# Gathering four blocks of tokens with sixteen matmuls in a row, in the gate projection's banks

## The chip, the cores and the metric

The kernel runs on one NeuronCore of a Trainium2 chip. The metric is the device time of one execution in microseconds (us); runs of a kernel are compared by their median. The profile is of one execution, and all times in it are us from the span's start unless marked ns.

## The reference

The program is one layer of a hybrid backbone over 512 latent tokens of 1024 channels with 256 context tokens: adaptive RMSNorm, one input projection, a bidirectional state-space scan and a gated MLP as parallel branches, an output projection, and then a mixture of experts. Only the last matters here:

```python
def expert_choice_ffn(xn, router_w, w_gate, w_up, w_down):
    b, n, d = xn.shape
    cap = CAPACITY_FACTOR * n // N_EXPERTS          # 64 tokens for each of 16 experts
    logits = jnp.einsum('bnd,de->ben', xn, router_w).astype(jnp.float32)
    aff = jax.nn.softmax(logits, axis=1)
    gate, idx = lax.top_k(aff, cap)
    xg = jax.vmap(lambda xs, ix: xs[ix])(xn, idx)
    hid = jax.nn.silu(jnp.einsum('becd,edf->becf', xg, w_gate)) * jnp.einsum('becd,edf->becf', xg, w_up)
    y = jnp.einsum('becf,efd->becd', hid, w_down) * gate[..., None].astype(xn.dtype)
    scatter = lambda ix, ys: jnp.zeros((n, d), ys.dtype).at[ix.reshape(-1)].add(ys.reshape(-1, d))
    return jax.vmap(scatter)(idx, y)
```

Each of the 16 experts picks 64 of the 512 tokens, runs a SwiGLU of width 1024 on them, and adds the weighted result back to these tokens. All weights are float32.

## The kernel before

All stages up to the router come first and are not touched. The expert stage runs over 8 pairs of experts (`for pr in range(NE // 2)`, L1129). The 128 tokens of a pair (64 for each expert) lie side by side as columns. For one pair, in the order of TensorE's queue:

- gate projection `pg = project("pg", ...)` (L1086): 8 steps `kt` over 128 input channels each; in every step four calls, for two halves of the 1024 outputs and two experts. One call is a matmul with 64 columns of weights loaded and 512 columns streamed; the trace shows each float32 call as two records. Between the steps the results of the pair before are added to their tokens (`to_their_tokens`, L1117, run from `between`).
- `route` (L1059): the pair's gate values and the transposed one-hot matrix `oh`.
- up projection `pu` (L1142), 64 records in a row; VectorE and ScalarE meanwhile form silu of the gate, and VectorE multiplies it by `pu` (L1144).
- the gather of the next pair's tokens, `channels` (L1074): for each of 8 blocks of 128 channels (`k`), four matmuls over the four tiles of 128 tokens (`x2`, shown as `F` in the trace) with the one-hot matrix `ot`, 128x128 each (eight records), and one ScalarE activation that scales and shifts the block with `mcol` and writes it to `xg` (shown as `m`). It comes in two halves of four blocks; behind each half stand four transposes of the hidden values (L1154) and a ScalarE copy of these into `ht` (L1155).
- the down projection `down` (L1156), two column halves of 32 records each, evacuated by VectorE (L1170) and split in two parts for the scatter.

The matmuls of this stage are kept in program order (`matmul`, L1042). PSUM has eight banks of 512 float32 columns: pool `pw` gives `x` two buffers, `pd` two, and `pg` and `pu` one buffer of two banks each. The four blocks of a half lie in one `x` bank, 128 columns apart, and the program lets TensorE write the next block to that bank only when ScalarE has read the last one.

For pair 0 there is no pair before it in which to gather. `first_tokens` (L1106) gathers two blocks ahead of every second step of the gate projection, and before step 6 also runs `places_of` (L1049), eight small matmuls that turn VectorE's top-k result into the slots of all other pairs.

Weights come by DMA from SyncE's queue (`expert_pieces`, L662, line L673 in the trace), in pieces of 1 MiB: 24 in a pair, two experts alternating, 8 for gate, 8 for up and 8 for down; in the last pair the down pieces are four of 1 MiB, four of 0.75 and four of 0.25. They go round 19 slots in SBUF (5 and 6 named `e`, 2 `w`, 6 `f`): a piece is requested when TensorE has read the last matmul of the piece 19 places before it. The first 19 are requested before the expert stage starts, the other 173 MiB as slots come free. Nothing else moves by DMA in this stage but the output at the end.

Of the kernel before, what the change touches and what calls it, by code (L numbers as in the profile page):

```python
# [7 lines left out]
F32 = mybir.dt.float32  # L8
# [4 lines left out]
AF = mybir.ActivationFunctionType  # L13
# [7 lines left out]
NT = 4  # L21
# [12 lines left out]
def tile_backbone(  # L34
# [7 lines left out]
    V, S, G, T = nc.vector, nc.scalar, nc.gpsimd, nc.tensor  # L42
# [127 lines left out]
    with tc.tile_pool(name="st", bufs=2) as st:  # L170
# [81 lines left out]
        for kt in range(NK):  # L252
            p = aux()
# [3 lines left out]
        for k2 in range(NK // 2):  # L257
            p = aux()
# [112 lines left out]
    for o, n, parts in ((0, 512, (xT,)), (512, 256, (xch.bitcast(F32), xcl.bitcast(F32)))):  # L371
        p = acc()[:, :n]
        ops = [(k, a) for k in (0, 4) for a in parts]
        for i, (k, a) in enumerate(ops):
            for q in range(4):
                T.matmul(p[32 * q:32 * q + 32, :], dtw[:, k + q, :], a[:, k + q, :],
                         start=i == 0, stop=i == len(ops) - 1)
        V.tensor_scalar(dth[:, o:o + n], p, dtb[:, 0:1], None, op0=OP.add)
    p = aux()
# [24 lines left out]
    p = aux()  # L404
# [11 lines left out]
    p = aux()  # L416
# [123 lines left out]
    def steps(gen, n):  # L540
        for _ in range(n):
            next(gen, None)
# [213 lines left out]
    for h in range(2):  # L756
        p = aux()
# [4 lines left out]
        p = aux()  # L762
# [7 lines left out]
    for m, wh, wl in ahead(cols(W, 3104)):  # L770
        pu = acc()
# [4 lines left out]
        for t in range(NT):  # L776
            T.matmul(pm[:, 128 * t:128 * t + 128], vt[:, t, 128 * m:128 * m + 128], wst[:, m, :],
                     start=True, stop=True)
# [15 lines left out]
    for m, is_gate, wh, wl in ahead(pairs(cols(W, 6176), cols(w_pb.rearrange("l k n -> (l k) n"), 0))):  # L794
        p = acc()
# [38 lines left out]
    for m, wh, wl in ahead(cols(W, 5152)):  # L834
        p = acc()
# [4 lines left out]
    for g in range(NG):  # L840
        p = aux()
# [8 lines left out]
    x2 = big.tile([128, NT, 1024], F32, name="F")  # L850
# [6 lines left out]
    for m, wh, wl in ahead(cols(w_pa.rearrange("l k n -> (l k) n"), 0)):  # L857
        p = acc()
# [17 lines left out]
    def full(name, bufs=1):  # L876
        return rp.tile([128, 1024], F32, name=name, bufs=bufs)
# [8 lines left out]
    mcol = rp.tile([128, 32], F32, bufs=1)  # L886
# [125 lines left out]
    pw = ctx.enter_context(tc.tile_pool(name="pw", bufs=2, space=PSUM))  # L1012
# [10 lines left out]
    p = pw.tile([128, 512], F32, name="pd")  # L1023
    for t in range(NT):
        T.transpose(p[:16, 128 * t:128 * t + 128], aff[:, t, :], ident)
    xg, ot = full("m1").rearrange("p (k n) -> p k n", k=NK), pick(rank)
# [15 lines left out]
    def matmul(*a, **k):  # L1042

        return tc.keep_in_program_order(T.matmul(*a, **k))  # L1044
# [4 lines left out]
    def places_of():  # L1049
        p = pw.tile([128, 512], F32, name="pd")  # L1050
        for k, a in enumerate((chosen, count)):
            for t in range(NT):
                matmul(p[:, 64 * k + 16 * t:64 * k + 16 * t + 16], a[:, 128 * t:128 * t + 128], i16,
                         start=True, stop=True)
        st_ = slott.rearrange("p t e -> p (t e)")
        S.copy(st_, p[:, :64])
        V.tensor_mul(st_, st_, p[:, 64:128])
# [13 lines left out]
        S.copy(oh, p)  # L1071
        return oh, gi

    def channels(xt_, ot, ks):  # L1074

        p = pw.tile([128, 512], F32, name="x")
        for j, k in enumerate(ks):
            o = p[:, 128 * j:128 * j + 128]
            for t in range(NT):
                matmul(o, x2[:, t, 128 * k:128 * k + 128], ot[:, t, :], start=t == 0, stop=t == NT - 1)  # L1080
            S.activation(xt_[:, k, :], o, AF.Identity, scale=mcol[:, 8 + k:9 + k], bias=mcol[:, k:k + 1])  # L1081

    def tokens():
        return full("m1").rearrange("p (k n) -> p k n", k=NK)
# [1 line left out]
    def project(name, op, between=lambda i: None):  # L1086
        p = pw.tile([128, 2, 512], F32, name=name, bufs=1)
        for kp in range(4):
            w = None
            for k in range(2):  # L1090
                kt = 2 * kp + k
                if pr == 0:
                    between(kt)
                w = w or [piece() for _ in range(2)]
                for hf in range(2):
                    for e in range(2):
                        matmul(p[64 * e:64 * e + 64, hf, :], op[:, kt, 64 * e:64 * e + 64],
                                 w[e][:, k, 512 * hf:512 * hf + 512], start=kt == 0, stop=kt == NK - 1)
                if pr:
                    between(kt)  # L1100
        return p

    fin = rp.tile([128, 8, NT], F32, name="rst")
    q = [fin[:, k, :] for k in range(8)]

    def first_tokens(kt):  # L1106
        if kt % 2 == 0:
            if kt == 6:
                places_of()
            channels(xg, ot, (kt, kt + 1))  # L1110

    def halves_of(hi, lo, c0, a):

# [14 lines left out]
    behind_ = iter(())  # L1128
    for pr in range(NE // 2):  # L1129
        last = pr == NE // 2 - 1  # L1130
        if pr == 0:
            pg = project("pg", xg, first_tokens)
        else:
            pg = project("pg", xg, lambda kt: steps(behind_, 1))
        oh, gi = route(pr, ot)
        if not last:
            ot = pick(slott[:, :, 2 * pr + 2:2 * pr + 4])
# [7 lines left out]
        if not last:  # L1145
            xg = tokens()
        ht = full("m2").rearrange("p (k n) -> p k n", k=NK)
        for hf in range(2):
            if not last:
                channels(xg, ot, range(4 * hf, 4 * hf + 4))  # L1150
            b = gs[hf]
            p = pw.tile([128, 512], F32, name="x")
            for k in range(4):
                transpose(p[:, 128 * k:128 * k + 128], b[:, 128 * k:128 * k + 128], ident)  # L1154
            S.copy(ht[:, 4 * hf:4 * hf + 4, :], p.rearrange("p (k n) -> p k n", k=4))  # L1155
        def down(c0, c1, nk, behind=None):  # L1156
            pd = pw.tile([128, 512], F32, name="pd", bufs=2)[:, :c1 - c0]
            for k0 in range(0, NK, nk):
                w = [piece() for _ in range(2)]
                with tc.issue_after(behind.ins) if behind and (k0 or c0 > 512) else nullcontext():  # L1160
                    for k in range(nk):
                        kt = k0 + k
                        for e in range(2):
                            (T.matmul if last else matmul)(pd[64 * e:64 * e + 64, :], ht[:, kt, 64 * e:64 * e + 64], w[e][:, k, :],  # L1164
                                     start=kt == 0, stop=kt == NK - 1)
            return pd
# [104 lines left out]
```

## Time and profile before

| | |
|---|---|
| time of the runs, median of 3 | 1179.45 us (1177.4 to 5647.97) |
| the profiled execution | 1177.17 us |
| its span, first to last instruction | 1175.4 us |
| TensorE (PE) busy | 1081.8 us, 92% of the span |
| weight loads (PEld), VectorE (DVE), ScalarE (ACT) | 61%, 49%, 29% |
| mean granted TensorE clock | 0.990 |

PE is TensorE's matmuls, PEld its weight loads, DVE VectorE, ACT ScalarE, SPq SyncE's DMA queue. Busy time is a union of the instructions' spans; matmuls are pipelined, so the end of one lies behind the start of the next. "x8" in a row counts merged records. In square brackets stands the idle time before an instruction and what released it.

### The profile page before, as it was taken

Reading aid. Unit: us, or ns where it says so; the run is one execution under the profiler, and the core shown is the slowest. Engines: PE = TensorE matmul, PEld = TensorE weight load, DVE = VectorE, ACT = ScalarE, POOL = GpSimd, SP = SyncE. Lnnn points to the kernel's source line nnn. Section 1 sums busy time; section 2 is a strip of 40 time slices with the busy share of each in tenths; the row PEclk is TensorE's granted clock in tenths of the full one; section 3 lists DMA queues with packets and bytes.
Section 4 is the critical chain, followed back from the end, with each engine's and each line's share of the span. In section 5 each row is a group of like instructions: output and inputs, shape, how many; then the busy total and the mean of one; then the engine's idle time right before and its main releaser. Section 6 shows DMA issues by size and latency. Waiting matters only on the chain.

```text
span 1175.4 us, 15016 instructions
## 1 busy us (share of the span) xinstructions
PE 1081.8 (92%) x5939; PEld 711.1 (61%) x5939; DVE 579.6 (49%) x1061; ACT 339.1 (29%) x645; POOL 66.4 (6%) x58
## 2 busy tenths in 40 slices
PE   2999899899999999999999699999898989899995
PEld 1778777799788888687897344343434343434333
DVE  2768999988797556536644711212030302121215
ACT  4343756553343223324333211010101010101002
POOL 2002232321000000100000000000000000000000
PEclk9999999999999999999999799999999999999998
DMA  9941624232576575525282898999999999999951
GB/s 213 248 121 54 200 90 161 73 108 73 179 219 210 191 241 186 173 74 177 72 326 97 298 374 314 395 406 393 407 393 409 393 408 396 405 397 402 402 182 72
DMA packets 149663, 291.85 MB, mean 248 GB/s; under 512 B 8468, under 2 KB 75188, under 8 KB 149592
## 3 DMA queue, kind: packets, MB, share of 16 engines
q1 hardware_dynamic: 149224, 290.79, 69.1%
q0 software_dynamic: 288, 0.07, 0.7%
q8 instruction: 47, 0.77, 0.3%
q14 instruction: 24, 0.20, 0.1%
q10 hardware_dynamic: 80, 0.02, 0.0%
HBM read 288.67 MB, written 2.18 MB: 247 GB/s over the span
## 4 chain that ended last, share of the span: by engine, by line
PE 78%; DVE 11%; ACT 4%; DMA 4%; issue 2%; POOL 0%; SPq 0%; DVEq 0%; ACTq 0%
PE x L1044 10%; PE pg L1044 10%; PE pu L1044 9%; PE pd L1044 8%; PE acc L358 7%; PE acc L360 7%; PE acc L359 7%; PE acc L603 2%; PE acc L601 2%; PE acc L602 2%; ACT m L1081 2%; DMA aw<-in_ada_w_dram 2%; PE pd L1164 1%; DVE gq L515 1%; DVE wl L74 1%
## 5 line engine op out<-in xcount | busy, mean ns | idle before, releaser
L358 PE MATMUL acc<-xmh,wh 128*128 128x512 f32 x352 | 139.1, 395 | 0.0
L359 PE MATMUL acc<-xml,wh 128*128 128x512 f32 x352 | 139.0, 395 | 0.0
L360 PE MATMUL acc<-xmh,wl 128*128 128x512 f32 x352 | 138.1, 392 | 0.0
L73 ACT CAST wh<-w 128x1024 fp32r<-128x1024 f32 (+1 forms) x84 | 84.4, 1005 | 170.5 <-PE acc L359 133.3
L74 DVE TENSOR_TENSOR wl<-w,wh 128x1024 fp32r<-128x1024 f32 (+1 forms) x81 | 95.8, 1183 | 68.2 <-ACT wh L73 67.2
L1170 DVE SCALAR_TENSOR_TENSOR t<-pd,gi,m 128x512 f32<-128x512 f32 (+2 forms) x17 | 12.2, 719 | 178.5 <-PE pd L1044 167.7
L1044 PE MATMUL x<-ot,F 128*128 128x128 f32 x512 | 74.9, 290 | 26.1 <-ACT m L1081 25.3
L1044 PEld LDWEIGHTS x<-ot,F 128*128 128x128 f32 x512 | 62.7, 193 | 44.1 <-ACT m L1081 36.6
L1125 DVE TENSOR_TENSOR F<-F,x 128x512 f32<-128x512 f32 x56 | 38.5, 688 | 91.2 <-PE x L1044 90.7
L1081 ACT ACTIVATE m<-x,mcol 128x128 f32<-128x128 f32 x64 | 29.3, 457 | 177.0 <-PE x L1044 177.0
L1044 PE MATMUL pg<-e,m 128*64 128x512 f32 x296 | 76.4, 602 | 0.0
L360 PEld LDWEIGHTS acc<-xmh,wl 128*128 128x128 f32 x352 | 66.3, 188 | 14.9 <-issue 1.2
L358 PEld LDWEIGHTS acc<-xmh,wh 128*128 128x128 f32 x352 | 66.3, 188 | 14.7 <-ACT wh L73 0.8
L601 PE MATMUL acc<-wh,xmh 128*128 128x256 f32 x256 | 73.5, 287 | 1.0 <-DVE F L614 1.0
L359 PEld LDWEIGHTS acc<-xml,wh 128*128 128x128 f32 x352 | 66.3, 188 | 13.1 <-issue 0.4
L603 PE MATMUL acc<-wl,xmh 128*128 128x256 f32 x256 | 73.3, 286 | 0.6 <-DVE wl L74 0.6
L1044 PE MATMUL pu<-e,m 128*64 128x512 f32 x304 | 73.7, 594 | 0.0
L602 PE MATMUL acc<-wh,xml 128*128 128x256 f32 x256 | 72.5, 283 | 0.0
L1044 PE MATMUL pd<-e,m 128*64 128x512 f32 x280 | 66.6, 594 | 0.0
L1144 DVE TENSOR_TENSOR t<-t,pu 128x512 f32<-128x512 f32 x16 | 10.3, 684 | 95.9 <-PE pu L1044 95.9
L358 PE MATMUL acc<-rh,wh 128*128 128x512 f32 x128 | 50.4, 396 | 0.8 <-ACT rh L73 0.5
L603 PEld LDWEIGHTS acc<-wl,xmh 128*128 128x128 f32 x256 | 49.0, 191 | 3.4 <-issue 2.5
(398 smaller groups left out, 1892.4 us busy)
## 6 DMA issues: line engine op xcount, KB each, us to landing
e<-in_w_up_dram SPq DMA_DIRECT2D x38, 1024.0 KB
e<-in_w_gate_dram SPq DMA_DIRECT2D x37, 1024.0 KB
e<-in_w_down_dram SPq DMA_DIRECT2D x35, 1024.0 KB
w<-in_w_in_dram SPq DMA_DIRECT2D x23, 1024.0 KB
f<-in_w_down_dram SPq DMA_DIRECT2D x20, 1024.0 KB
f<-in_w_up_dram SPq DMA_DIRECT2D x19, 1024.0 KB
f<-in_w_gate_dram SPq DMA_DIRECT2D x19, 1024.0 KB
e<-in_ada_w_dram SPq DMA_DIRECT2D x32, 512.0 KB
```

Source lines behind the costliest of these rows:

```text
L73: S.copy(hi, src)
L74: (lo_eng or V).tensor_sub(lo, src, hi.bitcast(F32))
L358: T.matmul(p, wh[:, kt, :], rh[:, kt, :], start=kt == 0, stop=False)
L359: T.matmul(p, wh[:, kt, :], rl[:, kt, :], start=False, stop=False)
L360: T.matmul(p, wl[:, kt, :], rh[:, kt, :], start=False, stop=kt == NK - 1)
L601: T.matmul(pp[t], lh[:, kt, a], wh[:, k, :], start=kt == 0, stop=False)
L602: T.matmul(pp[t], ll[:, kt, a], wh[:, k, :], start=False, stop=False)
L603: T.matmul(pp[t], lh[:, kt, a], wl[:, k, :], start=False, stop=kt == NK - 1)
L1044: return tc.keep_in_program_order(T.matmul(*a, **k))
L1081: S.activation(xt_[:, k, :], o, AF.Identity, scale=mcol[:, 8 + k:9 + k], bias=mcol[:, k:k + 1])
L1125: V.tensor_add(h[:, t, c0:c0 + 512], h[:, t, c0:c0 + 512], p)
L1170: V.scalar_tensor_tensor(a, pd, gi[:, 0:1], g2k[:, c0:c1], op0=OP.mult, op1=OP.mult)
```

## The change

`channels` takes a bank as an argument and issues all sixteen matmuls of four blocks first, then the four activations. The bank is no longer one of `x`: for the next pair's gather the two halves use the two banks of a `pg` buffer, for the first pair's those of a `pu` buffer. The two groups of transposes and their copies now stand together between the halves' matmuls. The first pair's eight blocks are all gathered ahead of the gate projection; `places_of` moves behind step 6's matmuls. `project` calls `between` behind a step's matmuls in every pair.

```diff
--- before.py
+++ after.py
@@ -1071,14 +1071,17 @@
         S.copy(oh, p)
         return oh, gi
 
-    def channels(xt_, ot, ks):
-
-        p = pw.tile([128, 512], F32, name="x")
-        for j, k in enumerate(ks):
-            o = p[:, 128 * j:128 * j + 128]
+    def channels(xt_, ot, hf, p):
+
+        for j in range(4):
+            k = 4 * hf + j
             for t in range(NT):
-                matmul(o, x2[:, t, 128 * k:128 * k + 128], ot[:, t, :], start=t == 0, stop=t == NT - 1)
-            S.activation(xt_[:, k, :], o, AF.Identity, scale=mcol[:, 8 + k:9 + k], bias=mcol[:, k:k + 1])
+                matmul(p[:, 128 * j:128 * j + 128], x2[:, t, 128 * k:128 * k + 128], ot[:, t, :],
+                       start=t == 0, stop=t == NT - 1)
+        for j in range(4):
+            k = 4 * hf + j
+            S.activation(xt_[:, k, :], p[:, 128 * j:128 * j + 128], AF.Identity, scale=mcol[:, 8 + k:9 + k],
+                         bias=mcol[:, k:k + 1])
 
     def tokens():
         return full("m1").rearrange("p (k n) -> p k n", k=NK)
@@ -1089,25 +1092,20 @@
             w = None
             for k in range(2):
                 kt = 2 * kp + k
-                if pr == 0:
-                    between(kt)
                 w = w or [piece() for _ in range(2)]
                 for hf in range(2):
                     for e in range(2):
                         matmul(p[64 * e:64 * e + 64, hf, :], op[:, kt, 64 * e:64 * e + 64],
                                  w[e][:, k, 512 * hf:512 * hf + 512], start=kt == 0, stop=kt == NK - 1)
-                if pr:
-                    between(kt)
+                between(kt)
         return p
 
     fin = rp.tile([128, 8, NT], F32, name="rst")
     q = [fin[:, k, :] for k in range(8)]
 
-    def first_tokens(kt):
-        if kt % 2 == 0:
-            if kt == 6:
-                places_of()
-            channels(xg, ot, (kt, kt + 1))
+    first_banks = pw.tile([128, 2, 512], F32, name="pu", bufs=1)
+    for hf in range(2):
+        channels(xg, ot, hf, first_banks[:, hf, :])
 
     def halves_of(hi, lo, c0, a):
 
@@ -1128,10 +1126,7 @@
     behind_ = iter(())
     for pr in range(NE // 2):
         last = pr == NE // 2 - 1
-        if pr == 0:
-            pg = project("pg", xg, first_tokens)
-        else:
-            pg = project("pg", xg, lambda kt: steps(behind_, 1))
+        pg = project("pg", xg, lambda kt: places_of() if pr == 0 and kt == 6 else steps(behind_, 1))
         oh, gi = route(pr, ot)
         if not last:
             ot = pick(slott[:, :, 2 * pr + 2:2 * pr + 4])
@@ -1145,14 +1140,17 @@
         if not last:
             xg = tokens()
         ht = full("m2").rearrange("p (k n) -> p k n", k=NK)
+        if not last:
+            gather = pw.tile([128, 2, 512], F32, name="pg", bufs=1)
+            channels(xg, ot, 0, gather[:, 0, :])
         for hf in range(2):
-            if not last:
-                channels(xg, ot, range(4 * hf, 4 * hf + 4))
             b = gs[hf]
             p = pw.tile([128, 512], F32, name="x")
             for k in range(4):
                 transpose(p[:, 128 * k:128 * k + 128], b[:, 128 * k:128 * k + 128], ident)
             S.copy(ht[:, 4 * hf:4 * hf + 4, :], p.rearrange("p (k n) -> p k n", k=4))
+        if not last:
+            channels(xg, ot, 1, gather[:, 1, :])
         def down(c0, c1, nk, behind=None):
             pd = pw.tile([128, 512], F32, name="pd", bufs=2)[:, :c1 - c0]
             for k0 in range(0, NK, nk):
```

How the instructions stand now. On TensorE, between the up and the down projection of pair 0 (`x` and `pg` are PSUM, `ot` the one-hot matrix, `F` the tokens, `ident` the transposes' identity; in brackets the engine whose semaphore is waited for), before, from the gather's third block to the first half's transposes:

```order
L1044 MATMUL x<-ot,F 128x128 [waits Activation_49]
L1044 MATMUL x<-ot,F 128x128 x3
L1044 MATMUL x<-ot,F 128x128 [waits Activation_49]
L1044 MATMUL x<-ot,F 128x128 x3
L1047 MATMUL x<-ident,t_5841 128x128 [waits DVE_49]
L1047 MATMUL x<-ident,t_5841 128x128 x3
```

And now, from the first of the gather to the first down matmul:

```order
L1044 MATMUL pg<-ot,F 128x128 [waits DVE_49,PE_49]
L1044 MATMUL pg<-ot,F 128x128 x15
L1047 MATMUL x<-ident,t_5838 128x128 [waits DVE_49]
L1047 MATMUL x<-ident,t_5838 128x128 x3
L1047 MATMUL x<-ident,t_5839 128x128 [waits DVE_49,Activation_49]
L1047 MATMUL x<-ident,t_5839 128x128 x3
L1044 MATMUL pg<-ot,F 128x128 [waits Activation_49]
L1044 MATMUL pg<-ot,F 128x128 x15
L1044 MATMUL pd<-f,m_5896 64x512 [waits DMAHW4_49,Activation_49]
```

Sixteen matmuls stand together where four stood, and the waits for ScalarE between blocks are gone. One is left on the second half's first matmul: by its semaphore count it is for the fourth activation of the first half. The wait ahead of the second transposes is for a ScalarE instruction of before the up projection, that ahead of the down projection for the first copy of `ht`.

On ScalarE at the same place, from the first block's activation to the first part of the scatter, before:

```order
L1081 ACTIVATE m_5898<-x,mcol 128x128 [waits PE_49,Activation_49]
L1081 ACTIVATE m_5898<-x,mcol 128x128 [waits PE_49] x3
L1155 COPY m_5899<-x 128x512 [waits PE_49]
L1081 ACTIVATE m_5898<-x,mcol 128x128 [waits PE_49] x4
L1155 COPY m_5899<-x 128x512 [waits PE_49]
L73 CAST t_5979<-t_5981 128x512 [waits DVE_49]
```

And now:

```order
L1083 ACTIVATE m_5895<-pg,mcol 128x128 [waits PE_49,Activation_49]
L1083 ACTIVATE m_5895<-pg,mcol 128x128 x3
L1151 COPY m_5896<-x 128x512 [waits PE_49] x2
L1083 ACTIVATE m_5895<-pg,mcol 128x128 [waits PE_49]
L1083 ACTIVATE m_5895<-pg,mcol 128x128 x3
L73 CAST t_5975<-t_5977 128x512 [waits DVE_49]
```

Only the first activation of four waits for TensorE (for the sixteenth matmul, by its count); the two copies stand together ahead of the second half's activations.

On TensorE at the start of pair 0, the sum of the rows before (with -) and now (with +):

```order
 L1025 MATMUL pd<-ident,aff 16x128 x4
-L1044 MATMUL x<-ot,F 128x128 x8
-L1044 MATMUL pg<-e,m_5697 64x512 x8
-L1044 MATMUL x<-ot,F 128x128 x8
-L1044 MATMUL pg<-e,m_5697 64x512 x8
-L1044 MATMUL x<-ot,F 128x128 x8
-L1044 MATMUL pg<-e,m_5697 64x512 x8
+L1044 MATMUL pu<-ot,F 128x128 x32
+L1044 MATMUL pg<-e,m_5697 64x512 x28
 L1044 LDWEIGHTS t_5717
```

The gather's 32 matmuls stand ahead of the gate projection, of which 28 now come before the slots' matmuls. SyncE's queue holds the same transfers in the same order.

## Rows read from the trace of the kernel before

**Rows 1.** The page: busy time; then DMA engines' busy tenths in 40 slices.

```profile
PE 1081.8 (92%) x5939; PEld 711.1 (61%) x5939; DVE 579.6 (49%) x1061; ACT 339.1 (29%) x645; POOL 66.4 (6%) x58
DMA  9941624232576575525282898999999999999951
```

**Rows 2.** Chain of waits, pair 1's up projection to down projection: start, us, what.

```profile
748.40 13.88 PE pu L1044 x64
762.28 1.10 PE x L1044 x8
...
775.75 13.88 PE pd L1044 x64
```

**Rows 3.** Timeline, pair 1's gather: start, us, engine, line, what, idle before.

```profile
762.21 1.16 PE L1044 MATMUL x<-ot,F 128*128 128x128 f32 x8
762.36 1.28 DVE L1144 TENSOR_TENSOR t<-t,pu 128x512 f32<-128x512 f32 x2 [12.11 <-PE pu L1044]
763.41 0.46 ACT L1081 ACTIVATE m<-x,mcol 128x128 f32<-128x128 f32 x1 [13.89 <-PE x L1044]
763.92 1.16 PE L1044 MATMUL x<-ot,F 128*128 128x128 f32 x8 [0.55 <-ACT m L1081]
...
768.33 0.60 PE L1047 MATMUL x<-ident,t 128*128 128x128 f32 x4
768.53 0.46 ACT L1081 ACTIVATE m<-x,mcol 128x128 f32<-128x128 f32 x1 [1.25 <-PE x L1044]
768.96 0.59 ACT L1155 COPY m<-x 128x512 f32<-128x512 f32 x1
769.04 1.16 PE L1044 MATMUL x<-ot,F 128*128 128x128 f32 x8
```

**Rows 4.** Window over pair 6's gather, L1044 alone: us, PE, PEld busy, clock, DMA.

```profile
1075.90:1089.40 13.50, 9.29 (x68) 7.77 (x66) 1.00 1.03 409
```

**Rows 5.** PE's timeline near the end; instructions of tile x (ns least/median/most).

```profile
1161.28 1.95 PE L1232 MATMUL pg<-ident,mcol 128*128 128x128 f32 x16
...
L1044 PE MATMUL x<-ot,F x512: 275/275/470, 657.5 to 1088.7; 128*128 128x128 f32 x171
```

**Rows 6.** Timeline of PE, and one row of DVE, in the first pair's gate projection.

```profile
657.45 1.96 PE L1044 MATMUL x<-ot,F 128*128 128x128 f32 x8
...
661.05 3.65 PE L1044 MATMUL pg<-e,m 128*64 128x512 f32 x16
...
677.40 0.35 PE L1044 MATMUL pd<-i,t 16*128 16x16 bf16 x8
...
684.06 1.05 PE L1044 MATMUL x<-aff,ot 128*128 128x2 f32 x8
...
670.09 1.21 DVE L1039 TENSOR_TENSOR_SCAN t<-t 16x512 bf16<-16x512 bf16 x1
```

**Rows 7.** Windows: us, PE, PEld, DVE, ACT, POOL busy, clock, DMA share, GB/s.

```profile
661.40:666.60 5.20, 4.65 (x26) 2.09 (x23) 4.98 (x11) 0.67 (x2) 0.00 (x0) 1.00 0.16 11
712.00:718.40 6.40, 6.40 (x36) 2.70 (x36) 0.00 (x0) 1.02 (x2) 0.00 (x0) 1.00 0.08 16
...
726.90:789.60 62.70, 59.30 (x296) 25.34 (x292) 11.97 (x19) 7.71 (x15) 0.00 (x0) 1.00 1.03 400
1040.60:1103.30 62.70, 59.30 (x294) 25.32 (x292) 11.97 (x19) 7.70 (x15) 0.00 (x0) 1.00 1.03 401
...
1132.50:1137.50 5.00, 5.00 (x26) 1.72 (x24) 0.00 (x0) 0.00 (x0) 0.00 (x0) 1.00 0.00 0
```

**Rows 8.** Chain of waits in the last pair's down projection: start, us, what.

```profile
1140.83 7.14 PE pd L1164 x32
...
1157.05 1.91 PE pd L1164 x28
```

**Rows 9.** Windows around the first block of the gather, columns as in rows 7.

```profile
650.00:657.40 7.40, 1.68 (x9) 0.97 (x8) 6.76 (x17) 0.31 (x1) 0.00 (x0) 0.50 1.04 392
...
659.40:660.00 0.60, 0.05 (x2) 0.04 (x1) 0.57 (x3) 0.46 (x1) 0.00 (x0) 0.97 1.01 403
```

## The prediction

> **What bounds the kernel now.** I read the page's busy shares and slices first. TensorE is busy 92% of the span, and in the last third of the span the DMA engines are 90% busy or more slice after slice [rows 1]. The change lies wholly in the expert stage, so two questions decide: which of the two ends last there, and what TensorE waits for.
>
> The chain of waits answers the first. Through the expert stage it runs on TensorE, and in each pair of experts it has the same piece between the last up matmul and the first down matmul: in pair 1 from 762.28 to 775.75, 13.47 us [rows 2]. The timeline of that piece [rows 3] is to be read row by row: a block of the gather (8 matmul records) starts at 762.21 and is over at 763.37; ScalarE evacuates it from 763.41 for 0.46; the next block starts at 763.92, released by that evacuation. Block follows block every 1.71 us. The four transposes at 768.33 fill part of one such wait. The window over pair 6 says that it is the same later: the gather 9.29 of 13.5 us busy, clock 1.00 [rows 4].
>
> How short could a block be? The sixteen 128x128 matmul records in a row at the end took 1.95 us [rows 5]; less one record's 0.275, that is 15 steps of 0.1117. Eight steps are 0.89, so 0.81 of each 1.71 is the wait, with the drain and refill that the idle column (0.55) leaves out.
>
> The second question is whether weights arrive in time. They move at 400 to 401 GB/s with the engines at 1.03 in the windows of pairs 1 and 6 [rows 7]: the transfers run at their own pace. But they are early: nothing moves any more from 1132.5 on, and the last weights are first used at 1157.05 [rows 7, 8]. TensorE is named by no row of the waits as waiting for a transfer in this stage. So TensorE ends last, with some 25 us in hand against the weights. That reserve is the second bound.
>
> **The change part by part.** *Gather of pairs 1 to 7* (seven times). Its 64 records and the 8 of the transposes stay; what changes is the number of waits. Counted from the first record: eight take 1.16 [rows 3], 24 more steps of 0.1117 make 3.84. By the built order the first evacuation waits for all sixteen matmuls, then four run without a wait. Evacuation to the next ScalarE row is 768.53 to 768.96, 0.43 [rows 3]; ScalarE starts 0.04 behind TensorE, so four end at 3.88 + 3 x 0.43 + 0.46 = 5.63. TensorE's eight transposes run meanwhile, to about 4.55. The second sixteen wait for the fourth evacuation although they write the other bank, and start at 5.68 (0.05 behind, as at 763.92): a new wait of 1.13 where there were seven, six of 0.81 and one of 0.38. Then 32 records to 9.36, and about 0.1 to the down matmul: 9.45 against 13.47, **4.02 us a pair, 28.1 in seven**.
>
> What is queued behind that wait: only the second half and the down matmuls. ScalarE's two copies for the down matmuls stand behind the four evacuations and end near 6.8 (2 x 0.59), before 9.45. The second half's evacuations end 1.8 behind it, under 13.88 us of down matmuls, so the next gate projection finds them. If that cover were gone they would cost 1.8. VectorE's products, the transposes' input, take 1.28 from 762.36 [rows 3] and are ready before 765.9, when they are now wanted.
>
> *First pair.* Before, 657.45 to 684.06, 26.6 us, the blocks two by two between gate matmuls with a wait in each two [rows 6]. Now: the first eight at half clock end at 659.41 as before; 24 more at 0.1117 to 662.3; four evacuations and a restart, to 664.1; 32 more, to 667.8; the 64 gate records, priced as the 64 of the up projection [rows 2], 13.9; the routing matmuls 0.3. End near 682.0: **2.1 saved**. VectorE has the routing's input by 671.3 [rows 6], so moving it behind a projection step costs nothing.
>
> *Sum for TensorE:* 28.1 + 2.1 = 30.2; the span would be 1145.2.
>
> *Weights.* Every slot is refilled when TensorE has read it, so the moved gather moves transfers too. The first gate pair was read by 664.7 (661.05 + 3.65) and the queue, dry until then, moved again from 666.6 [rows 6, 7]. Now that reading ends at 667.8 + 13.9/4 = 671.3 and the queue restarts near 673.5, 6.9 later (6.6 worked out, with a little for the first gate matmul's own start). In return it doesn't run dry again as it did from 712 to 718.4 [rows 7]: the slot that it lacked comes 6.1 us sooner, so it could go on at 712.3, and by then (38.8 us of transfers) 14.8 of the 16 pieces ahead are done. What lies behind the first 19 pieces is 173 MiB, 181.4 MB, at 400.5 GB/s 453.0 us without a gap: the last lands at 1126.5, which was 1132.5. The tightest piece is the second half of the last pair's first down part: 4 MiB (10.5 us) land behind it, so it lands at 1116.0. It was used half of 7.14 us behind 1140.83 [rows 8], 31.0 before the end. With that the span can't be under 1116.1 + 31.0 = **1147.1**. So TensorE alone would end 1.9 us sooner than the weights let it, and the weights decide by a hair.
>
> The profiled execution is 1177.17 with a span of 1175.4, 1.8 outside it; it lies 0.2 under the lowest run and 2.3 under the median shown. 1147.1 + 1.8 is **1149**, 28.2 less, 2.4%.
>
> The Trainium skill speaks against a gain here: DMA: Bandwidth & Descriptors, "Where 436 GB/s comes from", has HBM to SBUF bound near 358 GB/s. By that the 181.4 MB would take 507 us and the same sum would be 1201. The trace differs, 400 to 401 in the windows of both pairs [rows 7], and the measurement decides.
>
> **Unknown costs, from both sides.** No row shows 32 gather records in a row. Pace 0.1117 (sixteen in a row, rows 5) or 0.137 (1.10 for eight in the chain, rows 2, which holds a start): I take the first, being nearest in kind; the second takes 64 x 0.026 x 7 = 11.4 back. Nor does it show four evacuations in a row: 0.43 apart, or 0.51 with a hand-over like 763.37 to 763.41 each: 0.24 x 7 = 1.7 back. If the second sixteen waited for nothing, 1.1 x 7 more, but the weights then hold the span at 1147.1. Weights 1% slower than 400.5 (the pair windows differ by a quarter of that): 4.5 back. 1% faster: TensorE decides, 1147.0.
>
> **The rivals.**
> *A. The weights run slower once TensorE drains its reserve.* For it: the engines at 1.03 have no room, and at 1116 the reserve is gone. Against: their pace is the same in pairs 1 and 6. At 1 to 2% less, 1153.5 to 1158. With the Trainium skill's 358 it would be the 1201 above, which the trace all but rules out (0.01 of A's chance).
> *B. The gather is slower than the sum has it* (pace 0.137, or evacuations 0.51 apart): 30.2 - 11.4 = 18.8 saved, 1158; then the weights don't bind.
> *C. The transfers bind already and the gain is given back.* For it: DMA share 1.03. The time stays at 1177, or rises by the 6.9 of the late restart to 1184. Against: 25 us lie between the end of the transfers and the last first use [rows 7, 8].
> *D. Slower: TensorE's clock falls in the longer wait.* Before the gather it was busy 1.68 of the 7.4 us to 657.4, and the granted clock stood at 0.50, the lower of its two levels (1.2 of 2.4 GHz); it came back with the first block [rows 9]. If a wait of 1.1 (1.8 in the first pair) made it fall, the 72 records of a gather would take 0.1117 more each, 8.0 us, against 4.0 saved: 28 us more in seven, 1205. It decides from a half of the gather at the lower level on. Against: seven waits within 13.5 us now leave 1.00 in pair 6 [rows 4], and the total idle falls. The Trainium skill bears on this: TensorE: Matmul & The Clock Gate, "A second HAM failure mode: psum-queue depth-cycling", tells of short idles between matmul groups at which the clock swings. The trace of before, with its seven waits a pair, doesn't show it.
>
> **How the numbers follow.** Forecast 0.65 (1146 to 1152.5); A 0.13; B 0.11; C 0.06; D 0.05. Time 1149. The range reaches from 1145 (evacuations and weights both kind) over all of A and B to 1159, leaving out C and D, 0.11, and a little at each end. About 2%, 1153.6 and 1200.7, is what a measurement of this kernel can tell from no change. Faster by over 2%: the forecast, about half of A and a little of B, 0.75; within: the rest of A and B, C, 0.20; slower: D, 0.05.
>
> **What would show it.** In the changed trace: two runs of 32 gather records a pair, each near 3.8 us; four evacuations 0.43 to 0.46 apart; one TensorE wait of about 1.1 between transposes and the second run; last up to first down 9.4 to 9.5; pair period 58.7 instead of 62.7; DMA still near 400 GB/s and done near 1126; small TensorE waits on weights in the last pair alone. The forecast is wrong if a wait on weights stands before the last pair, if the 32 take 4.4, or if a clock under 1.00 stands between 670 and 1120.

## The result, and the profile after

The changed kernel takes 1150.36 us (median of four runs, 1149.88 to 1151.37), the kernel before 1177.4 beside it (median of its runs without one of 5647.97): ratio 0.977, 95% interval 0.975 to 0.980. That is 27 us and 2.3% less. The forecast was 1149.0 with a range of 1145 to 1159. The profiled execution is 1151.37, its span 1149.6.

The page of the changed kernel: busy times, the DMA slices, and the shares of the chain by engine.

```profile
PE 1070.2 (93%) x5939; PEld 709.5 (62%) x5939; DVE 579.2 (50%) x1061; ACT 331.9 (29%) x645; POOL 66.2 (6%) x58
...
DMA  9941634231476566622464669999999999999994
...
PE 74%; DVE 11%; DMA 7%; ACT 4%; issue 3%; POOL 1%; SPq 0%; DVEq 0%; ACTq 0%; POOLq 0%
```

TensorE's share rose by one point only; the last third of the slices is as full of transfers as in [rows 1].

The gather of pair 1 in the chain of waits, to be set against [rows 2]:

```profile
755.37 3.78 PE pg L1044 x32
759.16 0.02 issue
759.18 1.51 ACT m L1083 x4
760.69 0.04 issue
760.73 3.84 PE pg L1044 x32
764.57 0.57 PE pd L1044
```

From 755.37 to 764.57 are 9.20 us where 13.47 stood: 4.27 saved in this pair, 29.9 in seven. TensorE's and then ScalarE's timeline of the same piece, against [rows 3] (idle time and its releaser in brackets):

```profile
755.30 3.84 PE L1044 MATMUL pg<-ot,F 128*128 128x128 f32 x32
758.98 1.04 PE L1047 MATMUL x<-ident,t 128*128 128x128 f32 x8
760.73 3.84 PE L1044 MATMUL pg<-ot,F 128*128 128x128 f32 x32 [0.72 <-ACT m L1083]
```

```profile
759.18 1.50 ACT L1083 ACTIVATE m<-pg,mcol 128x128 f32<-128x128 f32 x4 [16.57 <-PE pg L1044]
760.56 1.08 ACT L1151 COPY m<-x 128x512 f32<-128x512 f32 x2
764.61 1.50 ACT L1083 ACTIVATE m<-pg,mcol 128x128 f32<-128x128 f32 x4 [2.97 <-PE pg L1044]
```

Thirty-two records take 3.84 and four evacuations 1.50; one wait is left, 0.72 in its row.

The first pair, TensorE's timeline, against [rows 6]:

```profile
655.90 5.78 PE L1044 MATMUL pu<-ot,F 128*128 128x128 f32 x32
663.33 3.84 PE L1044 MATMUL pu<-ot,F 128*128 128x128 f32 x32 [1.64 <-ACT m L1083]
...
681.42 1.05 PE L1044 MATMUL x<-aff,ot 128*128 128x2 f32 x8
```

From the first gather record to the routing matmuls are 25.5 us (681.42 - 655.90) where 26.6 stood. The first 32 records needed 5.78, the second 3.84. The windows say why, and how the transfers went (columns as in [rows 7]; the last three are the granted clock, the DMA share and GB/s):

```profile
657.00:660.00 3.00, 3.00 (x16) 3.00 (x15) 2.86 (x7) 0.00 (x0) 0.00 (x0) 0.50 0.58 223
660.00:661.00 1.00, 1.00 (x11) 1.00 (x10) 0.96 (x2) 0.00 (x0) 0.00 (x0) 0.93 0.00 0
661.00:673.00 12.00, 10.36 (x67) 6.21 (x67) 8.38 (x17) 3.00 (x8) 0.00 (x0) 1.00 0.06 16
720.00:778.50 58.50, 57.78 (x294) 24.97 (x292) 11.96 (x19) 6.88 (x15) 0.00 (x0) 1.00 1.03 401
1012.00:1070.60 58.60, 57.88 (x294) 25.07 (x292) 11.95 (x19) 6.89 (x15) 0.00 (x0) 1.00 1.03 401
1130.00:1132.00 2.00, 2.00 (x26) 1.46 (x24) 0.54 (x1) 0.00 (x0) 0.00 (x0) 1.00 0.00 0
```

The clock stood at 0.50 (1.2 of 2.4 GHz) for four microseconds of the gather. The transfers were all but at rest from 661 to 673, then ran at 401 GB/s as before, and were done by 1130, where 1126 was forecast. A pair takes 58.5 us now, so TensorE uses up its reserve of weights and meets them in the last pair. Its timeline there:

```profile
1101.18 3.22 PE L1044 MATMUL pu<-e,m 128*64 128x512 f32 x13 [0.91 <-DMA e<-in_w_up_dram]
...
1106.30 3.65 PE L1044 MATMUL pu<-w,m 128*64 128x512 f32 x14 [1.47 <-DMA w<-in_w_up_dram]
...
1118.51 3.65 PE L1162 MATMUL pd<-f,m 128*64 128x512 f32 x16 [1.57 <-DMA f<-in_w_down_dram]
```

The last pair, from its first gate matmul in the chain (1070.78) to the end, takes 78.8 us; before it was 72.1. So the span's 25.8 us come together as 29.9 from seven gathers, 1.1 from the first pair, 1.6 from a stage that began sooner in this execution (655.90 against 657.45, an early part that the change doesn't touch), and -6.7 for weights.

### The profile page after: what moved, and what is told of

Same layout as the page of the kernel before. It is cut to its first block, busy times and chain, and to the rows that moved or that the text cites. A ratio compares the mean times of both kernels' runs of the same rounds, so it can differ in the third digit from the quotient of the medians.

```text
span 1149.6 us, 15045 instructions
## 1 busy us (share of the span) xinstructions
PE 1070.2 (93%) x5939; PEld 709.5 (62%) x5939; DVE 579.2 (50%) x1061; ACT 331.9 (29%) x645; POOL 66.2 (6%) x58
## 4 chain that ended last, share of the span: by engine, by line
PE 74%; DVE 11%; DMA 7%; ACT 4%; issue 3%; POOL 1%; SPq 0%; DVEq 0%; ACTq 0%; POOLq 0%
PE pg L1044 15%; PE pu L1044 10%; PE pd L1044 8%; PE acc L358 7%; PE acc L360 7%; PE acc L359 7%; PE x L1044 4%; PE acc L603 2%; PE acc L601 2%; PE acc L602 2%; DMA w<-in_w_up_dram 2%; DMA aw<-in_ada_w_dram 2%; DVE wl L74 1%; ACT m L1083 1%; DVE gq L515 1%
## 5 line engine op out<-in xcount | busy, mean ns | idle before, releaser
L1044 PE MATMUL pg<-e,m 128*64 128x512 f32 x296 | 76.0, 602 | 0.0
L1044 PE MATMUL pu<-e,m 128*64 128x512 f32 x304 | 74.8, 595 | 0.9 <-DMA e<-in_w_up_dram 0.9
L1044 PE MATMUL pd<-e,m 128*64 128x512 f32 x280 | 66.6, 594 | 0.0
L1083 ACT ACTIVATE m<-pg,mcol 128x128 f32<-128x128 f32 x56 | 21.0, 456 | 135.9 <-PE pg L1044 135.9
L1044 PEld LDWEIGHTS pg<-ot,F 128*128 128x128 f32 x448 | 51.1, 192 | 12.5 <-ACT m L1083 6.8
L1044 PE MATMUL pg<-ot,F 128*128 128x128 f32 x448 | 53.7, 279 | 5.1 <-ACT m L1083 5.1
```

What stands on the lines that cost most here:

```text
L1083: S.activation(xt_[:, k, :], p[:, 128 * j:128 * j + 128], AF.Identity, scale=mcol[:, 8 + k:9 + k], bias=mcol[:, k:k + 1])
```

## The experiments

Theory W: the gathers and the first pair save TensorE more than the time shows, and the weights take the rest back in the last pair. Rival R: the time follows TensorE's saving, and the last pair is longer for another reason. All ratios are to the kernel before on the same chip.

| kernel | median us | ratio, 95% interval |
|---|---|---|
| changed kernel again | 1151.18 | 0.978, 0.976 to 0.980 |
| pairs only | 1150.68 | 0.978, 0.976 to 0.981 |
| first pair only | 1173.85 | 0.998, 0.996 to 1.000 |
| no wait for the second sixteen | 1150.63 | 0.978, 0.976 to 0.981 |
| changed, half the weights' bytes | 1143.26 | 0.971, 0.969 to 0.973 |
| no wait, half the bytes | 1135.26 | 0.965, 0.963 to 0.967 |
| before, half the bytes | 1175.29 | 0.998, 0.997 to 1.000 |
| single banks | 1151.27 | 0.978, 0.975 to 0.980 |
| first pair two blocks ahead | 1146.39 | 0.973, 0.971 to 0.976 |
| the same, no wait | 1145.64 | 0.974, 0.971 to 0.976 |
| the same, TensorE kept busy ahead | 1143.67 | 0.972, 0.970 to 0.974 |
| changed kernel, third time | 1148.65 | 0.975, 0.973 to 0.978 |

### The changed kernel again, and its two parts

> The changed kernel once more, beside its parts. Expected: 0.977 of before, 1150 us. Theory W (the weights cap the end): the gather of each of seven pairs is 4.3 us shorter on TensorE and the first pair's piece 1.0 us, but the last pair takes 78.8 us from its first gate matmul to the end where it took 72.1, waiting for its up and down pieces. If the first pair's matmuls again take 5.8 us for the first 32 records with the granted clock back only 4 us behind their start, that is the change's own doing and not one run's; if they take 4.9, it was chance.

Measured: 1151.18. The first 32 records took 5.54; in all eight traces of kernels with this first pair it was 4.83 to 6.06. So the slow start is neither a constant nor one run's mishap: it depends on how long after the gather's first record the clock comes back.

For the pairs alone the first pair stays in its old form, with `between` ahead of the step in pair 0:

```diff
-    first_banks = pw.tile([128, 2, 512], F32, name="pu", bufs=1)
-    for hf in range(2):
-        channels(xg, ot, hf, first_banks[:, hf, :])
+    def first_tokens(kt):
+        if kt % 2 == 0:
+            if kt == 6:
+                places_of()
+            channels2(xg, ot, (kt, kt + 1))
```

> The change in the seven later pairs alone; the first pair gathers two blocks at a time between gate matmuls, as before. Theory W: TensorE loses the 1.0 us that the first pair gained, but the first gate pieces are read at about 665 instead of 671, so the weights start to move again some 6 us sooner; they may run dry for 2 or 3 us near 712. The last pair then waits 3 us or more less, and the time is 1147 to 1149, at or below the changed kernel. Rival R (the time follows TensorE's saving, the waits of the last pair come from something else): 1.0 more than the changed kernel, 1151.5.

Measured: 1150.68 (1149.03 to 1152.67), the changed kernel's time as far as the runs can tell. The 1147 to 1149 that I had drawn from theory W did not come: the restart did come sooner, but it bought nothing. The window of 70 us from the first gather record, of the changed kernel and then of this one:

```profile
655.90:725.90 70.00, 67.58 (x375) 34.52 (x376) 21.16 (x40) 10.20 (x24) 0.00 (x0) 0.97 0.83 324
```

```profile
655.73:725.73 70.00, 67.02 (x361) 33.55 (x362) 20.11 (x39) 10.87 (x24) 0.00 (x0) 0.95 0.85 322
```

324 and 322 GB/s: in the same time as much was moved. With the old first pair TensorE reads the gate pieces over 28.7 us (this execution's first gather record to routing, again with a late clock), so the queue ran dry again between them (DMA share 0.38 from 660 to 670, 0.90 and 0.92 in the two tens behind it, 0.82 from 710 to 720). So theory W is to be counted from how many bytes have moved by the time the queue stays full, and not from when it starts. I read this out of the run after its result; the versions at the end put it to the test.

> The change in the first pair alone; the seven later gathers go block by block as before. Both theories: the weights have 25 us in hand, so the restart of the transfers that comes 6 us later costs nothing, and the time is that of before less 1.0, some 1177 to 1178 (ratio 0.998 to 1.000). If the later restart cost something by itself, 1180 to 1184 (ratio above 1.002).

The edit is the other half of the diff. Measured: 1173.85, ratio 0.998 (0.996 to 1.000), some 2.4 us less than before and more than the 1.0 expected. In the three traces with the old first pair the stretch from first gather record to routing is 26.6, 28.7 and 28.3; in the eight with the new one 24.6 to 25.8, 25.2 in the mean. The mean saving is 2.6, and the profiled pair with its 1.1 was the odd one. A restart that is late does no harm while 25 us are in hand.

### Is it the weights? The wait taken away, and the bytes halved

```diff
-            channels(xg, ot, 1, gather[:, 1, :])
+            channels(xg, ot, 1, pw.tile([128, 2, 512], F32, name="pu", bufs=1)[:, 1, :])
```

> The changed kernel with the second sixteen matmuls of each later gather in a buffer of their own (the up projection's, free by then), so that they no longer wait for the four evacuations of the first. Both: the TensorE wait between the transposes and the second sixteen (0.72 us of idle column, 1.0 with the refill) goes and last up to first down falls from 9.2 to about 8.2 us, in seven pairs. Theory W: the weights set the end, so the last pair waits 7 us longer and the time stays at that of the changed kernel, within 1 us. Rival R: 7 us less, 1143.

Measured: 1150.63, the changed kernel's time. The chain of waits in pair 1 has the two runs of 32 records with only the transposes between them:

```profile
750.92 3.77 PE pg L1044 x32
754.69 0.87 PE x L1047 x8
755.56 3.57 PE pu L1044 x32
759.13 3.15 PE pd L1044 x13
```

From 750.92 to 759.13 are 8.21 us where the changed kernel had 9.20. But TensorE's timeline now shows it waiting for weights in pair 6 already:

```profile
1034.84 3.66 PE L1044 MATMUL pu<-e,m 128*64 128x512 f32 x16 [0.94 <-DMA e<-in_w_up_dram]
1039.98 3.65 PE L1044 MATMUL pu<-e,m 128*64 128x512 f32 x14 [1.48 <-DMA e<-in_w_up_dram]
```

One microsecond less in each of seven gathers, and not one in the time: what TensorE saved, it waits for weights a pair earlier. That is theory W.

```diff
+                    n += 1
+                    nl = nk if n <= 19 else nk // 2
-                    load(w, dram(exw[m], (e * 1024 + k * 128) * 1024 + c0,
-                                 [[1024, 128], [128 * 1024, nk], [1, c1 - c0]]))
+                    load(w[:, :nl, :], dram(exw[m], (e * 1024 + k * 128) * 1024 + c0,
+                                 [[1024, 128], [128 * 1024, nl], [1, c1 - c0]]))
+                    w = Half(w, nl)
```

`Half` lets the matmuls of step k read step k % nl of the piece.

> The changed kernel with half the bytes of every expert piece behind the 19th left out (half of those weights are not loaded; the matmuls read the loaded half twice, in the same number and shape). Theory W: the waits of the last pair vanish, it takes 72.1 us again instead of 78.8, and the time is 1150.4 less 6.7, that is 1143 to 1144.5; every gather is as in the changed kernel. Rival R (the last pair is longer for another reason than the weights' lateness): 1150, with the last pair near 78.

> The same half of the bytes left out, and the second sixteen matmuls in a buffer of their own, without the wait. Theory W: with the weights out of the way the removed wait shows in the time: 1.0 us in each of seven pairs less than with half the bytes alone, 1136 to 1137.5. Rival (the wait's time turns up elsewhere on TensorE, for instance in the down matmuls waiting for ScalarE's copies): no gain, 1143 to 1144.

> The kernel before with the same half of the bytes left out. Theory W: the weights set nothing there, 25 us in hand, so the time stays within 1 us of before, 1177 to 1179. Rival C (transfers bind already, or their traffic slows TensorE or the evacuations): 1170 or less. The difference between this and the changed kernel with half the bytes is then TensorE's whole saving, 33 to 34 us by theory W (30.9 from the gathers and about 1.5 to 2 that differ from run to run).

Measured: 1143.26, 1135.26 and 1175.29. With half the bytes the changed kernel is 7 us faster, in the expected band, and no transfer stands in its chain in the last pair:

```profile
1091.00 13.91 PE pu L1055 x64
1104.91 0.02 issue
1104.93 0.70 DVE t L1150
```

The 64 up records now run in one piece of 13.91, and the last pair takes 70.8 us instead of 78.8. Without the wait as well it is 8.0 us faster again, 0.7 below the band: the microsecond per gather that was worth nothing above is paid once the weights are out of the way. The kernel before gains 1.4 (0.998, 0.997 to 1.000); I had said within 1. Its last pair is 1.3 shorter (70.8), and the chain of waits shows the place: 42 down matmuls in a row ahead of the scatter, where the kernel before has 32 [rows 8] and then the evacuation of these by VectorE.

```profile
1139.02 9.02 PE pd L1175 x42
1148.04 0.43 PE pg L1199
```

So 1.3 of the gain in each of these kernels is another order at the end (those matmuls aren't held in program order) and not the weights; 6.7 of the 8.0 remains for these. Theory W stands and R falls.

### The banks

```diff
-            gather = pw.tile([128, 2, 512], F32, name="pg", bufs=1)
-            channels(xg, ot, 0, gather[:, 0, :])
+            channels(xg, ot, 0, pw.tile([128, 512], F32, name="x"))
...
-            channels(xg, ot, 1, gather[:, 1, :])
+            channels(xg, ot, 1, pw.tile([128, 512], F32, name="x"))
```

> The changed kernel with the sixteen matmuls of each later gather in the two single banks that the transposes use too, instead of the gate projection's pair. Sixteen in a row and four evacuations stay. Expected: the second four transposes now wait for the first half's evacuations and the second sixteen for the copy of the first transposes, about 0.5 us more a gather (9.7 instead of 9.2), 3.5 in seven; by theory W the weights hide that and the time is that of the changed kernel, 1150 to 1151. Rival (the choice of banks carries the gain): the gather is back above 12 us and the time above 1165.

Measured: 1151.27. TensorE's timeline of pair 1 in this kernel:

```profile
756.59 3.84 PE L1044 MATMUL x<-ot,F 128*128 128x128 f32 x32
760.26 0.60 PE L1047 MATMUL x<-ident,t 128*128 128x128 f32 x4
762.02 0.66 PE L1047 MATMUL x<-ident,t 128*128 128x128 f32 x4 [1.16 <-ACT m L1083]
762.51 3.71 PE L1044 MATMUL x<-ot,F 128*128 128x128 f32 x31
```

The gather takes 9.68 (756.66 to 766.34 in the chain), 0.5 more than in the changed kernel as worked out; the weights cover it. Sixteen in a row carry the shorter gather (13.47 before), the banks half a microsecond a pair that the time doesn't show.

### A version that beats both

If the weights set the end, the first pair is the place: what it delays, all later pieces have late. The first version gathers two blocks at a time into `x` banks, always two blocks ahead of the gate matmuls that use them (`blocks` is sixteen records and two evacuations):

```diff
+    def two_more():
+        k = next(ahead, None)
+        if k is not None:
+            blocks(xg, ot, (k, k + 1), pw.tile([128, 512], F32, name="x"))
+
+    two_more()
+    def first_tokens(kt):
+        if kt % 2 == 0:
+            two_more()
+            if kt == 6:
+                places_of()
```

> The later pairs as in the changed kernel; the first pair gathers two blocks at a time into banks of their own, always two blocks ahead of the gate matmuls that read them, so that TensorE waits for no evacuation there. Theory W (the weights set the end, counted from when their queue stops running dry): routing comes 23.8 us behind the first gather record instead of 25.6, the first gate pieces are read 9.3 us behind it instead of 15, the transfers start again 5 us sooner, lose about 1 us by running dry once more, and the time is 1145.5 to 1147. Rival, from the run with the first pair as before (its transfers started sooner as well, ran dry again and gave no gain): the queue runs dry again until the up pieces are read, nothing is gained, 1150 to 1151.

> The same first pair, and the later gathers' second sixteen in a buffer of their own, without the wait for the evacuations. Theory W: TensorE's further 7 us go into waits for weights, and the time is that of the version with the first pair alone, within 1 us (1145 to 1147). Rival: 7 us less than that one, 1139.

Measured: 1146.39 and 1145.64, as theory W had it; the two agree within 1 us although the second has the wait taken away in seven gathers, which was worth 8.0 us with half the bytes. The changed kernel beside them took 1148.65, so the gain over it is 2.3 and 3.0 us; the runs of the first (1143.66 to 1147.7) lie all below its runs (1148.06 to 1154.15), those of the second (1144.66 to 1148.85) overlap with them a little. TensorE's timeline of the first:

```profile
654.02 5.06 PE L1044 MATMUL x<-ot,F 128*128 128x128 f32 x32
659.01 3.65 PE L1044 MATMUL pg<-e,m 128*64 128x512 f32 x16
662.60 2.05 PE L1044 MATMUL x<-ot,F 128*128 128x128 f32 x16
664.58 3.65 PE L1044 MATMUL pg<-e,m 128*64 128x512 f32 x16
```

No bracket, so no wait; the first gate pieces are read 8.6 us behind the first gather record. Its window of 70 us moved 350 GB/s for the changed kernel's 324:

```profile
654.02:724.02 70.00, 69.22 (x383) 34.20 (x384) 21.57 (x41) 10.41 (x24) 0.00 (x0) 0.98 0.91 350
```

That is 1.8 MB more, 4.5 us of transfers at 401 GB/s; from the first gather record to the end this execution takes 490.0 us, the changed kernel's three 493.2 to 494.1.

The third version is the second with twelve matmuls on the identity behind the last matmuls ahead of the wait:

```diff
+    busy = aux()
+    with tc.issue_after(row.ins):
+        for _ in range(12):
+            T.matmul(busy[:, 0:128], ident, ident, start=True, stop=True)
```

> The last version, with twelve matmuls of the identity by itself (24 records, read by nobody) in the wait of 5.7 us ahead of the first gather. It tests the term of the first pair that was mis-sized: there the first 32 records took 4.8 to 6.1 us from run to run where 3.84 is the pace at full clock. If TensorE's being busy ahead of the gather brings the granted clock to 1.00 by its start, the first sixteen records take 1.95 to 2.1 us instead of 3.3 to 4, everything behind, the restart of the transfers too, comes about 2 us sooner, and the time is 2 us under the version before. If the clock stays at 0.50 until it has come back by itself: no change, or 0.5 us more.

> The changed kernel beside the three versions on the same chip: 0.978 of before, 1150 to 1151 us; 493 to 494 us from the first gather record to the end of the span.

Measured: 1148.65 for the changed kernel, 1.4 below the 1150 to 1151 expected of it, and 1143.67 (1143.14 to 1146.58) for this version beside it (1148.06 to 1154.15): 5.0 us or 0.4% less, and the runs of the two don't overlap. It is 2.0 under the version without the idle work, as expected, but the runs of these two overlap (1144.66 to 1148.85 without it), so this difference is not shown by the times alone. In the two profiled executions the stretch from the first gather record to the end is 486.2 us instead of 491.3. Its timeline and its windows:

```profile
649.05 3.56 PE L1014 MATMUL aux<-ident 128*128 128x128 f32 x24
654.98 0.60 PE L1029 MATMUL pd<-ident,aff 128*16 128x128 f32 x4 [2.37 <-DVE t L1007]
655.70 3.81 PE L1048 MATMUL x<-ot,F 128*128 128x128 f32 x32
```

```profile
649.00:650.00 1.00, 1.00 (x7) 1.00 (x6) 0.96 (x4) 0.00 (x0) 0.00 (x0) 0.50 1.01 389
650.00:651.00 1.00, 1.00 (x9) 1.00 (x8) 0.93 (x3) 0.00 (x0) 0.00 (x0) 0.73 1.04 389
651.00:652.00 1.00, 1.00 (x11) 1.00 (x10) 0.90 (x3) 0.00 (x0) 0.00 (x0) 1.00 1.06 389
653.00:655.60 2.60, 0.60 (x4) 0.30 (x4) 2.45 (x7) 0.00 (x0) 0.00 (x0) 1.00 1.05 385
655.70:725.70 70.00, 70.00 (x390) 33.65 (x392) 21.95 (x42) 10.42 (x24) 0.00 (x0) 1.00 0.94 363
```

The clock rose during the idle work and held over the 2.37 of waiting behind it, the first 32 records took 3.81 where they took 5.98 without the idle work, and the 70 us moved 363 GB/s instead of 349.

## Why the prediction was right, step by step

**The gather.** The pace taken from the sixteen records at the end [rows 5] was exact: 3.84 for 32. The wait that the built order showed was there. It came out shorter since four evacuations took 1.50, 0.35 apart, where I had 0.43 from an evacuation followed by a copy [rows 3]: 1.75. TensorE sat idle 0.72 and not 1.13, and a pair saved 4.27 and not 4.02. Both bounds that I had kept lay on the dear side; that an evacuation could follow its own kind faster than a copy follows an evacuation I didn't weigh.

**The first pair.** 2.1 was forecast, 1.1 seen in the profile, 2.6 in the mean of all traces. That the size was near is luck: I let the clock come back 2.0 us behind the first record because it had done so in one execution [rows 6, 9], and so had 4.85 us for the first 32 records. It came back 4.2 us behind it here, and the 32 records took 4.83 to 6.06. The old first pair was late in the same way in two of its three traces, so that the difference came out near all the same.

**TensorE alone** would therefore have ended sooner than the 1145.2 of the span forecast. With half the bytes the time is 1143.3, or 1144.6 with the 1.3 of the other order put back, against 1145.2 + 1.8 = 1147.0 by my sum.

**The weights.** That they would decide was the step that made the forecast good: by TensorE alone it would have come to 1144.6, nearly 6 us under what came. But "by a hair", 1.9 us of waiting, was mis-sized: 6.7 went to them. One part of this is that TensorE was quicker than the sum; that moves the wait and not the end. The other is the term "lands at 1116.0", and it does move the end. I took it from the bytes at the mean pace, and by bytes it came at 1115.1. That this is 0.9 sooner is luck again: the stage began 1.6 sooner in this execution, and the transfers started again at 672.0 and not at 673.5. A piece, though, is there when the last of the sixteen DMA engines has moved its share, and these had drifted apart. The sixteen landings of that piece (the trace records when each engine's share lands) lie between 1113.6 and 1118.5, the eighth at 1115.0; TensorE started again at 1118.51. With the 31.0 us behind it that gives 1149.5, and the span is 1149.6. In eight of the nine traces in which TensorE waits for weights the span ends 31.1 us behind the last landing of this piece, in the ninth (two blocks ahead, no wait) 32.7. Counted from the restart, the piece was there 446.5 us later where my sum had 442.5: 4.0 too late, of which the early start hid 1.5. In the same way an up piece, first share at 1102.8 and last at 1106.3, released the matmuls at 1106.30; the chain of waits names it:

```profile
1087.81 18.45 DMA w<-in_w_up_dram
```

How far the sixteen landings of one piece lie apart, mean over the pieces of a pair (24, in the last 28), and the most in the last pair:

| kernel | pairs 1 to 3 | pair 6 | last pair | most in it |
|---|---|---|---|---|
| before | 1.4 to 1.7 us | 2.3 | 2.2 | 2.3 |
| changed | 1.6 to 1.9 | 3.3 | 3.9 | 4.9 |
| first pair two blocks ahead | 2.6 to 2.8 | 4.1 | 4.6 | 5.7 |

The Trainium skill has the mechanism: by DMA: Bandwidth & Descriptors, "Why a DMA increments its semaphore by 16 and not by 1", every engine reports its own share and only all sixteen reports mean that the data is there. The landings in the trace agree (last one at 1118.46, TensorE at 1118.51); how far they lie apart is this case's number.

Why they drift apart was not tried by an experiment. It is not that the queue has no rests: in the kernel before the transfers ran at a share of 1.03 and 401 GB/s from 721 to 1103 too, and their landings stayed within 2.5 us. The trace shows that the drift grows in steps. In the changed kernel it goes from 1.8 to 3.2 us at 900.4 and from 3.5 to 4.8 at 1113.1, just ahead of the tightest piece; each step comes just behind a transfer of 16 KB that takes 1.1 us, at 896.3 and 1109.9, in the queue that the page lists as

```profile
q8 instruction: 47, 0.77, 0.3%
```

(packets, MB, share of the engines). In the eleven traces with all bytes, each of the 22 steps of over 0.4 us from one piece to the next, from 730 us on, comes within 4.4 us behind such a transfer; most of these transfers, some 26 us apart, are followed by no step. So the two agree in time, as if such a transfer held up one of the engines; no run moved or left out these transfers, and that they are the cause is not shown.

**The rivals.** A (weights slower): over whole pairs their pace stayed at 401 GB/s. From 1104 to 1122 it was 382, but the kernel before has 389 there, a difference of 0.3 us of transfers. The weights did cost more than forecast, by the drift. B (a slower gather): no, 3.84 and 1.50. C (transfers bind already): no; with half the bytes the kernel before gains 1.4, nearly all of it another order. D (the clock falls in the wait): no; it is 1.00 over whole pairs in the windows above, the longer wait included.

So of the two terms that were off, TensorE's end by 2.4 us and the tightest piece by 2.5, only the second reached the time: the profiled span is 2.5 over the 1147.1 of the forecast. The median of the runs lies 1.0 under the profiled execution and hides part of it.

Of the signs that I had listed, four came out otherwise: evacuations 0.35 apart and not 0.43 to 0.46, an idle wait of 0.72 and not 1.1, 9.20 us from last up to first down and not 9.4 to 9.5, transfers done at 1130 and not near 1126. The waits on weights stand in the last pair alone, as listed, but they are not small.

## What to carry to other kernels

When work on an engine is made shorter under a steady stream of weights, compute the second bound at once, and count a piece as there when the slowest DMA engine has moved its share: read from the trace how far the landings of one piece lie apart, at the end of the stream and not at its start. Once the stream bound here, nothing saved on TensorE counted but what let the queue stay full sooner: a first pair without waits and a TensorE kept at full clock ahead of it, while seven removed waits of a microsecond each gave nothing. A term read from a clock that had just come back is a draw from a range; take it from several executions or keep both ends.

## What the runs showed of the hardware that was not expected

- The drift of the DMA engines: at most 2.5 us between first and last landing of a piece in the kernel before and 4.9 in the changed one, at the same 401 GB/s. It grew in steps, each just behind a 16 KB transfer of the instruction queue; that this is the cause is not shown.
- The clock's return: behind TensorE's wait of 5.7 us the first 32 gather records took 4.83 to 6.06 us from one execution to the next, at 0.50 first and 1.00 then. In the one execution profiled with it, the clock rose to 1.00 by 651 during the 24 records of idle work, and it held through 2.37 us of waiting. The Trainium skill (TensorE: Matmul & The Clock Gate, "What's actually happening") says that the clock starts low and rises once TensorE is kept busy; the windows agree.
- ScalarE's evacuations of 128 columns in a row stand 0.35 us apart, and 0.46 is the duration of one: they overlap.
